# Sliding-window attention on Trainium2: from three float32r passes over 128-query blocks to plain float32 on four 64x64 tiles, with halves of 64 queries and 192 keys

## The chip, the cores and the metric

The kernel runs on one core of a Trainium2 chip. The time is device microseconds of one execution; the median of three runs of the kernel before is 2179.53 us (2178.03 to 2180.18).

The engines are called as in the profile: PE (TensorE; PEld is its loading of weights), DVE (VectorE), ACT (ScalarE), POOL (GpSimd) and SP (SyncE). Each works through its own instructions in order and waits for the others by semaphores.

## What is computed

A decoder layer over 2048 tokens of width 1024: one input product, then dilated window attention (16 heads of 64) beside a Mamba-2 mixer, an output product over both and a layer norm. The change concerns attention:

```python
for dilation in (1, 4, 16):          # query t sees t - j*dilation, j = 0..128
    scores = q . k - slope * distance            # q scaled by 1/8
    scores = where(0 <= steps <= 128, scores, -inf)
    lse = logsumexp(scores); p = exp(scores - lse); o = p @ v
y_att = sum over dilations of softmax(lse_1, lse_4, lse_16) * o
```

With dilation r the tokens fall into r subsequences, and each is cut into blocks of 128. A query sees at most 128 steps back, so a block of queries needs its own block of keys and the one before it.

## The kernel before, in words

**Products (to about 1250 us).** q, k, the gate z and the mixer's inputs come from one product in which every matmul is float32r with operands split in a high and a low part (three passes), arranged as seven products of 512-column halves; 44 jobs of two column tiles each. A result leaves PSUM by ACT (`ev<-pp`, L319) or DVE (L327), in tiles of the pool `ev` (six buffers), and `fin_qk` (L361) ends q and k: ACT rounds the scaled value into `hi` (L366), DVE forms the remainder (L367), and SP stores both (L369, L370) to `d_qh`, `d_ql`, `d_kh`, `d_kl`. The mixer's work is threaded between the products by the table `later`, keyed on a count of products. `copy_v` (L493) reorders V in DRAM for dilations 4 and 1 through POOL's queue, a token's row at a time.

**Attention (1250 to 1757 us).** Everything goes in pairs of heads: head h of a pair lies on partitions 64h to 64h+63. For each of 8 pairs, three dilations (d = 0 is dilation 16, d = 1 is 4, d = 2 is 1), four groups `qd` and two halves make 24 steps; a step takes two blocks of 128 queries for both heads. 192 steps in all. The order is written by hand (`manual_schedule`): in iteration i each engine gets `scores` of step i, `transposes` of step i-2 (TA = 2) and `values` of step i-3, then the odd jobs of that place.

- `scores` (L792): per block, q as weights of 64 rows and 128 columns, k as moving data of 256 columns (128 for a `first` block, which has no block before it: all of d = 0, the first of each subsequence otherwise), three passes (high-high, high-low, low-high) for two heads, into the banks `S` (pool `psS`, four). DVE then adds the bias table and takes the row minimum (L824), ACT exponentiates with the row sum (L832).
- `transposes` (L843): 128x128 pieces of P, four per key block, through the two banks `T` (`psT`), and one DVE copy (L854) per four into `PT`.
- `values` (L858): v as weights of 128 rows and 64 columns per head, PT moving, 128 columns; both heads side by side in a bank `N` (`psN`, two buffers), one bank for the four blocks of a group; ACT copies it to `num` when the group's second half is done (L877, L879, L882).
- `statistics` (L885) transposes minima and sums through an `N` bank after a dilation's end, `gather` and `weights` form the softmax over dilations, `combine` (POOL, for the last pair DVE) adds up.

q for d = 1 and d = 2 is permuted by POOL (`permute`, L773: high and low part, four pieces each). `load_qk` (L745) loads four arrays of 1 MB a pair on POOL's queue, `load_dil` (L753) the bias table (SP) and V (POOL). In the first four iterations `warm` (L836) adds eight matmuls on PE.

**Output (from 1757 us).** The product of both branches, split in high and low parts, four rows of tokens of the mixer's half first, then attention's half. Its weights are loaded by `load_w` on POOL's queue into buffers of attention as they come free.

Of the kernel before, what the change touches and what calls it, by code (L numbers as in the profile page):

```python
# [28 lines left out]
def hybrid_layer(ctx, tc, xT, xc, w52, wv, convw, convb, dtb, alog, dskp, gcol, wout,  # L29
# [15 lines left out]
    d_qh = [dtile(f"d_qh{i}", [128, S]) for i in range(8)]  # L45
    d_ql = [dtile(f"d_ql{i}", [128, S]) for i in range(8)]
    d_kh = [dtile(f"d_kh{i}", [128, S]) for i in range(8)]
    d_kl = [dtile(f"d_kl{i}", [128, S]) for i in range(8)]
# [37 lines left out]
    with ExitStack() as c1:  # L86
# [274 lines left out]
        def fin_qk(p, i, scale):  # L361
            dh, dl = (d_kh, d_kl) if scale == 1.0 else (d_qh, d_ql)

            def f(ci, q, e):
                hi = ev.tile([128, 512], F32R, name="ev")
                nc.scalar.activation(hi, e, AF.Copy, scale=scale)  # L366
                nc.vector.scalar_tensor_tensor(e, e, scale, hi.bitcast(F32), op0=OP.mult, op1=OP.subtract)  # L367
# [125 lines left out]
        def copy_v(d, b):  # L493

            o = (b % 4 * 512 + b // 4 * 32, 8 * b)[d - 1]
            nc.gpsimd.dma_start(d_v[d][b], dap(d_v[0], o * D, [[128 * D, (4, 16)[d - 1]], [D, (32, 8)[d - 1]], [1, D]]))
# [153 lines left out]
        with tc.manual_schedule(engines={E.PE, E.DVE, E.Activation, E.Pool}):  # L650
# [13 lines left out]
            for m, (ph, (kind, i)) in enumerate(jobs):  # L664
# [34 lines left out]
                elif kind == "z":  # L699
                    fin = fin_z(p, i)  # L700
                else:
                    fin = fin_qk(p, i, -0.125 if kind == "q" else 1.0)
# [23 lines left out]
    with ExitStack() as c2:  # L726
        qk = [c2.enter_context(tc.tile_pool(name="qk0", bufs=1, side="right", reuse_waits="tile"))]
        qq = c2.enter_context(tc.tile_pool(name="qq", bufs=1, side="right", reuse_waits="tile"))
        qk.append(c2.enter_context(tc.tile_pool(name="qk1", bufs=1, side="right", reuse_waits="tile")))
# [9 lines left out]
        def load_pair(pr):  # L739

            A = {"pr": pr, "num": [], "tab": {}, "v": {}, "q": {0: []}, "k": []}
# [3 lines left out]
        def load_qk(A):  # L745
            pr = A["pr"]
            for x, src, to in (("qh", d_qh, A["q"][0]), ("kh", d_kh, A["k"]),
# [95 lines left out]
        def transposes(d, qd, half, P):  # L843
            pts = {}
            for which in (0, 1):
                bl = [b for b in range(2) if which or not first(d, qd, 2 * half + b)]
                if not bl:
                    continue
# [410 lines left out]
```

## Time and profile before

| what | value |
|---|---|
| median of three runs | 2179.53 us |
| span of the profiled execution | 2166.2 us (mean granted clock 0.976) |
| outside the span (median less span) | 13.3 us |
| attention, first scores to last values | about 507 us of the span, 62.5 us a pair |
| PE busy in the whole span | 2045.6 us (94%) |
| DMA | 525.26 MB, mean 242 GB/s |

The median is of executions timed from outside; the profile gives the span from the first to the last instruction of one execution. The difference stands for what lies around it.

How to read the rows: a group (`--` by line) reads `line engine op out<-in shapes xcount | busy us, mean ns of one | idle before, what ended it`. A timeline row reads `start us, duration us, engine line op out<-in shapes xcount [idle before <- what ended it]`, and equal instructions that follow each other are merged, so the time from one row's start to the next tells more than a duration: a matmul's end is modelled, and it overlaps the next. A row of waits reads `engine line waited for: us in total, times, longest us`.

### The profile page before, as it was taken

Reading aid. Unit: us, or ns where it says so; the run is one execution under the profiler, and the core shown is the slowest. Engines: PE = TensorE matmul, PEld = TensorE weight load, DVE = VectorE, ACT = ScalarE, POOL = GpSimd, SP = SyncE. Lnnn points to the kernel's source line nnn. Section 1 sums busy time; section 2 is a strip of 40 time slices with the busy share of each in tenths; the row PEclk is TensorE's granted clock in tenths of the full one; section 3 lists DMA queues with packets and bytes.
Section 4 is the critical chain, followed back from the end, with each engine's and each line's share of the span. In section 5 each row is a group of like instructions: output and inputs, shape, how many; then the busy total and the mean of one; then the engine's idle time right before and its main releaser. Section 6 shows DMA issues by size and latency. Waiting matters only on the chain.

```text
span 2166.2 us, 38916 instructions
## 1 busy us (share of the span) xinstructions
PE 2045.6 (94%) x13856; PEld 1701.3 (79%) x13856; DVE 1393.9 (64%) x3145; ACT 1153.7 (53%) x3007; POOL 1089.8 (50%) x899
## 2 busy tenths in 40 slices
PE   7999998989999999979999999999999977999998
PEld 7998777768787787858888878788877865888886
DVE  3431554558999677735555568888888845655655
ACT  4231444435555676645766578888888841222221
POOL 2122545657687666655555331776566670422222
PEclk9999989999999999989999999999999988999999
DMA  9999778977678888898889863777776799222220
GB/s 330 373 334 339 231 256 283 326 282 225 190 223 292 307 319 299 286 399 285 278 281 289 290 233 94 226 217 225 231 224 184 206 367 283 98 102 84 97 82 29
DMA packets 260802, 525.26 MB, mean 242 GB/s; under 512 B 43713, under 2 KB 122689, under 8 KB 244609
## 3 DMA queue, kind: packets, MB, share of 16 engines
q1 hardware_dynamic: 181984, 255.37, 36.9%
q0 software_dynamic: 35280, 184.30, 24.0%
q10 hardware_dynamic: 43344, 83.12, 11.9%
q8 instruction: 109, 1.79, 0.3%
q14 instruction: 85, 0.69, 0.1%
HBM read 346.15 MB, written 193.33 MB: 249 GB/s over the span
## 4 chain that ended last, share of the span: by engine, by line
PE 47%; DMA 8%; DVE 4%; ACT 3%; issue 1%; ACTq 0%; POOL 0%; SPq 0%; DVEq 0%; POOLq 0%
PE S L816 6%; PE N L872 6%; PE T L852 6%; PE S L1032 4%; PE pp L310 3%; PE S L1034 3%; PE S L1033 3%; PE pp L314 3%; PE pp L312 3%; PE T L1032 2%; PE T L1033 2%; PE T L1034 2%; DMA kl<-d_kl 1%; DMA wb<-d_wd 1%; DVE P L824 1%
## 5 line engine op out<-in xcount | busy, mean ns | idle before, releaser
L266 POOL TENSOR_TENSOR w<-wr,w 128x512 fp32r<-128x512 f32 x231 | 353.8, 1548 | 183.9 <-ACT w L265 133.5
L832 ACT ACTIVATE P<-P,st 128x256 f32<-128x256 f32 (+1 forms) x768 | 345.1, 451 | 90.6 <-DVE st L824 90.1
L824 DVE CUSTOM_DVE_ANT_0 P<-S,tb 128x256 f32<-128x256 f32 (+1 forms) x768 | 235.4, 362 | 72.5 <-PE S L816 39.7
L319 ACT COPY ev<-pp 128x512 f32<-128x512 f32 x176 | 102.4, 582 | 184.2 <-PE pp L314 120.3
L854 DVE COPY PT<-T 128x512 f32<-128x512 f32 (+1 forms) x304 | 196.4, 677 | 4.0 <-PE T L852 4.0
L852 PE MATMUL T<-ident,P 128*128 128x128 f32 x1200 | 175.1, 282 | 6.0 <-DVE PT L854 6.0
L872 PE MATMUL N<-PT,v 128*64 128x128 f32 x2400 | 173.2, 281 | 0.0
L265 ACT CAST w<-wr 128x512 fp32r<-128x512 f32 x231 | 138.0, 618 | 51.9 <-DVE wr L258 35.1
L258 DVE TENSOR_TENSOR wr<-wr 128x512 f32<-128x512 f32 x132 | 143.1, 1084 | 15.2 <-POOL w L266 6.2
L872 PEld LDWEIGHTS N<-PT,v 128*64 128x64 f32 x2400 | 127.1, 136 | 32.1 <-issue 22.8
L852 PEld LDWEIGHTS T<-ident,P 128*128 128x128 f32 x1200 | 127.6, 140 | 30.0 <-DVE PT L854 7.4
L939 POOL TENSOR_TENSOR wb<-num,wb 128x2048 f32<-128x2048 f32 x21 | 96.3, 4587 | 98.6 <-DMA wb<-d_wd 54.5
L832 ACT ACTIVATION_READ_ACCUMULATOR P<-P,st 128x1 f32 x768 | 143.9, 187 | 0.0
L327 DVE TENSOR_TENSOR ev<-pp,ev 128x512 f32<-128x512 f32 x152 | 100.6, 682 | 54.1 <-PE pp L314 45.0
L816 PE MATMUL S<-kh,qp 64*128 64x256 f32 (+1 forms) x1024 | 124.4, 303 | 0.0
L1009 DVE TENSOR_REDUCE tb<-P 128x128 f32<-128x1024 f32 x32 | 64.0, 2000 | 85.2 <-PE N L1038 49.2
L416 DVE SCALAR_TENSOR_TENSOR acc<-U,cw,acc 128x2048 f32<-128x2048 f32 x36 | 111.2, 3089 | 4.5 <-ACT acc L413 4.1
L367 DVE SCALAR_TENSOR_TENSOR ev<-ev 128x512 f32<-128x512 f32 x64 | 64.2, 1015 | 66.6 <-ACT ev L366 66.6
L150 PE MATMUL pp<-vh,xh 128*128 128x256 f32 (+1 forms) x320 | 90.2, 289 | 15.1 <-ACT xh L173 15.0
L816 PEld LDWEIGHTS S<-kh,qp 64*128 64x128 f32 x1024 | 87.3, 185 | 21.5 <-issue 20.4
L143 POOL TENSOR_TENSOR vl<-vraw,vh 128x256 fp32r<-128x256 f32 (+1 forms) x32 | 30.1, 943 | 129.7 <-ACT vh L142 107.5
L1071 POOL TENSOR_TENSOR kh<-kh,wb 128x1024 f32<-128x1024 f32 x8 | 19.2, 2399 | 142.7 <-DVE kh L1070 142.7
(370 smaller groups left out, 6139.1 us busy)
## 6 DMA issues: line engine op xcount, KB each, us to landing
wr<-w ACTq DMA_DIRECT2D x157, 256.0 KB
v<-d_v POOLq DMA_DIRECT2D x24, 1024.0 KB, 7.1
wb<-d_wd SPq DMA_DIRECT2D x48, 512.0 KB
d_wc<-w SPq DMA_DIRECT2D x44, 512.0 KB
w<-d_wc POOLq DMA_DIRECT2D x44, 512.0 KB, 6.4
csb<-d_cs ACTq DMA_DIRECT2D x32, 512.0 KB
st<-xT SPq DMA_DIRECT2D x31, 512.0 KB
d_v<-vt SPq DMA_DIRECT2D x16, 512.0 KB
```

Of the source, the lines that this page charges most:

```text
L258: tt = lambda o, a, b, op=OP.subtract: nc.vector.tensor_tensor(q[o], q[a], q[b], op=op)
L265: nc.scalar.copy(t[:, 0], q[nm])
L266: nc.gpsimd.tensor_tensor(t[:, 1], q[nm], t[:, 0].bitcast(F32), op=OP.subtract)
L416: return lambda: nc.vector.scalar_tensor_tensor(acc[0], U[:, j:j + 16, :], cw[:, i, j:j + 1], acc[0], op0=OP.mult, op1=OP.add)
L816: nc.tensor.matmul(ov(sp[h][:, 256 * b:256 * b + w]), A["q"][d][x][hr, blk], kv(A["k"][y][hr]), start=(m == 0), stop=(m == 2))
L824: nc.vector.tensor_tensor_reduce(P[:, h, b, 256 - w:256], sp[h][:, c0:c0 + w], tab[:, h, tab.shape[2] - w:], 1.0, 3.0e38, OP.add, OP.min, ...
L832: nc.scalar.activation(p, p, AF.Exp, bias=stat(A, 0, d, h, blk), scale=-1.0, accum_out=stat(A, 1, d, h, blk))
L852: nc.tensor.transpose(tp[:, h, b], P[:, h, b, 128 * which:128 * which + 128], ident)
L854: nc.vector.tensor_copy(pt[:, :, bl[0]:2], tp[:, :, bl[0]:2])
L872: nc.tensor.matmul(nm[64 * h:64 * h + 64, bq * 128:bq * 128 + 128], v[:, k, 64 * h:64 * h + 64], pts[which][:, h, b], start=(f or not whic ...
L1032: nc.tensor.matmul(ps, uh[:, e, :], wh, start=(e == 0), stop=False)
L1033: nc.tensor.matmul(ps, uh[:, e, :], wl, start=False, stop=False)
```

## The change

q and k stay plain float32: `fin_qk` stores what the product gives, once, and the factor -1/8 is applied by DVE's bias instruction instead (its scale, with tables multiplied by -8). A pair loads two arrays, q and k, both double buffered, and POOL permutes one q per dilation.

A block of 128 queries is taken as two halves of 64. A half sees 192 keys: for the first half the two half blocks before it and its own, and likewise for the second. So the two halves see different windows, and each (head h, half a) gets its own 64x64 tile of PE: rows by h, columns by a. A step now takes blocks `half` and `2 + half` of a group instead of two neighbours; in the second of them the 192 columns lie at the other end of P (`cols`), so that the last 64 keys of the first and the first 64 of the second stand next to each other in columns 128 to 255 and are transposed together. That is four transposes of 128 keys and, in steps with a block of two key blocks, two of these shared ones, with a copy of half the width into `PC`. Values follow in two groups: 128 keys with 128 rows and 64 columns per head, moving 64 columns; then the remaining 64 keys on four tiles (rows by block, columns by head). Since a window begins at half blocks, V is also needed shifted by 64 rows: `vs`, loaded beside `v`, 15 blocks of it.

N becomes two banks, `N0` and `N1`, one for each of the step's blocks, used by a group of two steps and copied by two ACT copies of 256 columns, with one buffer each. The statistics are transposed through `T`. Within a subsequence block the tokens are reordered by half blocks, in `permute`, `copy_v` (pieces of 16 or 4 rows), the tables and the statistics. `load_w` names other buffers.

On PE a full step of attention (dilation 4) stood as follows; S are scores, T the transposes, N the values, kh and kl the parts of k, qp the permuted q, PT the transposed P:

```order
L816 MATMUL S<-kh,qp 128x4x2x32 x2
L816 MATMUL S<-kl,qp 128x4x2x32 x2
L816 MATMUL S<-kh,qp 128x4x2x32 x4
L816 MATMUL S<-kl,qp 128x4x2x32 x2
L816 MATMUL S<-kh,qp 128x4x2x32 x2
L852 MATMUL T<-ident,P 128x128 x8
L872 MATMUL N<-PT,v 64x128 x8
```

and stands now, in the same place (ex is the permuted q, PC the shared transposes, the two N the two banks):

```order
L812 MATMUL S<-k,ex 64x192 x8
L839 MATMUL T<-ident,P 128x128 x4
L847 MATMUL T<-ident,P 128x128 x2
L865 MATMUL N_13177<-PT,v 64x64 x2
L865 MATMUL N_13177<-PT,vs 64x64 x2
L865 MATMUL N_13178<-PT,vs 64x64 x2
L865 MATMUL N_13178<-PT,v 64x64 x2
L865 MATMUL N_13177<-PC,v 64x64 x2
L865 MATMUL N_13178<-PC,vs 64x64 x2
L865 MATMUL N_13177<-PC,vs 64x64 x2
L865 MATMUL N_13178<-PC,v 64x64 x2
```

Twelve score matmuls became eight, eight transposes six, and eight value matmuls sixteen of half the columns.

On ACT, at the end of dilation 4 and the beginning of dilation 1, the exponentials (P), the copies of N and that of the statistics (sT) stood like this:

```order
L879 COPY num<-N 128x16x32
L832 ACTIVATE P,st<-P,st 128x256 x8
L879 COPY num<-N 128x16x32
L892 COPY sT<-N 128x128
L832 ACTIVATE P,st<-P,st 128x256 x8
L882 COPY num<-N 128x4x16x8
```

and stand now:

```order
L892 COPY num<-N_17422 128x2x2x4x16
L892 COPY num<-N_17423 128x2x2x4x16
L824 ACTIVATE P,st<-P,st 128x192 x8
L892 COPY num<-N_17529 128x2x2x4x16
L892 COPY num<-N_17530 128x2x2x4x16
L907 COPY sT<-T 64x128
L908 COPY sT<-T 64x2x4x16
L824 ACTIVATE P,st<-P,st 128x192 x8
L895 COPY num<-N_17649 128x4x16x4
L895 COPY num<-N_17650 128x4x16x4
```

The exponentials keep their number at three quarters of the width, and each copy of N became two.

The core of the diff:

```diff
-        def fin_qk(p, i, scale):
-            dh, dl = (d_kh, d_kl) if scale == 1.0 else (d_qh, d_ql)
-
+        def fin_qk(p, i, to):
             def f(ci, q, e):
-                hi = ev.tile([128, 512], F32R, name="ev")
-                nc.scalar.activation(hi, e, AF.Copy, scale=scale)
-                nc.vector.scalar_tensor_tensor(e, e, scale, hi.bitcast(F32), op0=OP.mult, op1=OP.subtract)
-                s = slice(512 * (2 * p + q), 512 * (2 * p + q) + 512)
-                nc.sync.dma_start(dh[i + ci][:, s], hi.bitcast(F32))
-                nc.sync.dma_start(dl[i + ci][:, s], e)
+                s = 512 * (2 * p + q)
+                nc.sync.dma_start(to[i + ci][:, s:s + 512], e)
             return f
...
-        psN = c2.enter_context(tc.tile_pool(name="psN", bufs=2, space=PSUM, reuse_waits="tile"))
+        psN = c2.enter_context(tc.tile_pool(name="psN", bufs=1, space=PSUM, reuse_waits="tile"))
...
             v = A["v"][d] = io.tile([128, 16, 128], F32, name="v", bufs=3)
-            nc.gpsimd.dma_start(v, d_v[d][:, :, pr * 128:pr * 128 + 128].rearrange("b p e -> p b e"))
+            rows = lambda o, n, p: dap(d_v[d], o * D + pr * 128, [[D, p], [128 * D, n], [1, 128]])
+            nc.gpsimd.dma_start(v, rows(0, 16, 128))
+            if d:
+                vs = A["vs"][d] = io.tile([128, 16, 128], F32, name="vs", bufs=3)
+                nc.gpsimd.dma_start(vs[:, 0:15], rows(64, 15, 128))
...
+        def cols(d, qd, half, i):
+
+            w = 128 if first(d, qd, 2 * i + half) else 192
+            return slice(384 - w, 384) if i else slice(0, w)
...
+            for i in range(2):
+                blk, cs = 4 * qd + 2 * i + half, cols(d, qd, half, i)
+                for h in range(2):
+                    for a in range(2):
+                        o, kv = sp[h][64 * a:64 * a + 64, cs], keys(A, d, qd, 2 * i + half, h, a)
+                        if d:
+                            o = o.rearrange("p (c r j) -> p c r j", r=kv.shape[2], j=kv.shape[3])
+                        nc.tensor.matmul(o, A["q"][d][64 * h:64 * h + 64, blk, 64 * a:64 * a + 64], kv,
+                                         start=True, stop=True)
             for h in range(2):
...
+                    nc.vector.tensor_tensor_reduce(P[:, h, cs], sp[h][:, cs], t, -0.125, 3.0e38, OP.add, OP.min,
+                                                   accum_out=stat(A, 0, d, h, blk))
...
         def transposes(d, qd, half, P):
...
+            tp = psT.tile([128, 2, 2, 128], F32, name="T")
+            for h in range(2):
+                for i in range(2):
+                    nc.tensor.transpose(tp[:, h, i], P[:, h, 256 * i:256 * i + 128], ident)
+            pt = io.tile([128, 2, 2, 128], F32, name="PT", bufs=4)
+            nc.vector.tensor_copy(pt, tp)
+            new = [i for i in range(2) if not first(d, qd, 2 * i + half)]
+            if not new:
+                return pt, None
+            tc_ = psT.tile([128, 2, 2, 128], F32, name="T")
+            for h in range(2):
+                nc.tensor.transpose(tc_[:, 0, h], P[:, h, 128:256], ident)
+            pc = io.tile([128, 2, 128], F32, name="PC", bufs=2)
...
+                A["N"] = [psN.tile([128, 512], F32, name=f"N{i}") for i in range(2)]
...
+                for a in range(2):
+                    for h in range(2):
+                        w = (v, vs)[a != i][:, m - (a == i == 0 or a != i), 64 * h:64 * h + 64]
+                        mm(out(i, h, 64 * a, 64 * a + 64), w, pt[:, h, i, 64 * a:64 * a + 64], half == 0 and a == 0)
+            for a in range(2):
+                for i in range(2):
+                    m, rows = at(2 * i + half), slice(64 * i, 64 * i + 64)
+                    if first(d, qd, 2 * i + half):
+                        continue
+                    for h in range(2):
+                        w = v[rows, m - i] if a == i else vs[rows, m - 2 * i]
+                        mm(out(i, h, 64 * a, 64 * a + 64), w[:, 64 * h:64 * h + 64],
+                           pc[rows, h, 64 * a:64 * a + 64], False)
             if half == 1:
...
-            ps = psN.tile([128, 512], F32, name="N")
+            ps = psT.tile([128, 512], F32, name="T")
```

In the short steps, where `first` holds for both blocks, the scores are eight matmuls of 128 columns, the transposes four as before, and the values four matmuls of 128 columns as before.

More of the change, by code (lines that the diff above doesn't have):

```diff
@@ L43, in dtile @@
         return dram.tile(shape, F32, name=name, tag=name)
[L45 to L48, printed above, removed]
+    d_q = [dtile(f"d_q{i}", [128, S]) for i in range(8)]
+    d_k = [dtile(f"d_k{i}", [128, S]) for i in range(8)]
     d_za = [dtile(f"d_za{i}", [128, S]) for i in range(8)]
@@ L838, in warm @@
             ps = psT.tile([128, 512], F32, name="T")
[L839 to L840 removed]
+            x = A["k"]
+            for n in range(2):
                 nc.tensor.matmul(ps, x[:, 0, :], x[:, 4:8, :].rearrange("p r j -> p (r j)"), start=True, stop=True)
         def transposes(d, qd, half, P):
[L844 to L848, printed above, removed]
[L849 to L856 removed]
+            tp = psT.tile([128, 2, 2, 128], F32, name="T")
+            for h in range(2):
+                for i in range(2):
+                    nc.tensor.transpose(tp[:, h, i], P[:, h, 256 * i:256 * i + 128], ident)
[8 more added lines that the diff above has]
+            pc = io.tile([128, 2, 128], F32, name="PC", bufs=2)
+            rows = slice(64 * new[0], 128)
+            nc.vector.tensor_copy(pc[rows], tc_[rows, 0])
+            return pt, pc
         def values(A, d, qd, half, pts):
+            pt, pc = pts
             if half == 0:
@@ L862, in values @@
                     A["num"].append(cm_.tile([128, NR, NJ], F32, name="num", bufs=6))
-                A["N"] = psN.tile([128, 512], F32, name="N")
-            nm, num, v = A["N"], A["num"][d], A["v"][d]
-            for b in range(2):
-                bq = 2 * half + b
-                blk = 4 * qd + bq
-                f = first(d, qd, bq)
-                kb = blk - 4 if d == 1 else blk - 1
-                for k, which in ((blk, 1),) if f else ((kb, 0), (blk, 1)):
-                    for h in range(2):
-                        nc.tensor.matmul(nm[64 * h:64 * h + 64, bq * 128:bq * 128 + 128],
-                                         v[:, k, 64 * h:64 * h + 64], pts[which][:, h, b],
-                                         start=(f or not which), stop=bool(which))
@@ new lines, in values, with mm @@
+            num, v, vs = A["num"][d], A["v"][d], A["vs"].get(d)
+            at = lambda bq: 4 * bq + qd if d == 1 else 4 * qd + bq
+            out = lambda i, h, lo, hi: A["N"][i][64 * h:64 * h + 64, 128 * half + lo:128 * half + hi]
+            def mm(o, l, r, start):
+                nc.tensor.matmul(o, l, r, start=start, stop=True, skip_group_check=True)
+            for i in range(2):
+                m = at(2 * i + half)
+                if first(d, qd, 2 * i + half):
+                    for h in range(2):
+                        mm(out(i, h, 0, 128), v[:, m, 64 * h:64 * h + 64], pt[:, h, i], half == 0)
+                    continue
[3 more added lines that the diff above has]
+                        mm(out(i, h, 64 * a, 64 * a + 64), w, pt[:, h, i, 64 * a:64 * a + 64], half == 0 and a == 0)
@@ new lines, in values @@
+            for a in range(2):
+                for i in range(2):
+                    m, rows = at(2 * i + half), slice(64 * i, 64 * i + 64)
+                    if first(d, qd, 2 * i + half):
+                        continue
+                    for h in range(2):
+                        w = v[rows, m - i] if a == i else vs[rows, m - 2 * i]
+                        mm(out(i, h, 64 * a, 64 * a + 64), w[:, 64 * h:64 * h + 64],
+                           pc[rows, h, 64 * a:64 * a + 64], False)
@@ L1168, in hybrid_layer @@
                     residual(3)
-                    for e, name in enumerate(("num", "num", "num", "num", "qp", "v", "wb", "wb")):
+                    for e, name in enumerate(("num", "num", "num", "num", "vs", "v", "wb", "wb")):
                         load_w(e, name)
```

177 lines of the change are left out of this document (77 added, 100 removed).

## The prediction

> **What bounds the kernel now.** I read the page's first part, then the busy time in four stretches of the program, and then, inside the stretch that the change rewrites, the timeline of PE. The page:
>
> ```profile
> PE 2045.6 (94%) x13856; PEld 1701.3 (79%) x13856; DVE 1393.9 (64%) x3145; ACT 1153.7 (53%) x3007; POOL 1089.8 (50%) x899
> ```
>
> The stretches are the part of the products in which q and k are made and the state-space mixer runs (640 to 1000), attention (1250 to 1757), and the output stage. The columns are the stretch, its length, and busy time with instructions of PE, PEld, DVE, ACT and POOL, then granted clock, DMA share and GB/s.
>
> ```profile
> 640.00:1000.00 360.00, 333.22 (x1695) 271.63 (x1693) 246.82 (x336) 223.79 (x440) 233.41 (x184) 0.97 0.89 313
> 1250.00:1757.00 507.00, 499.96 (x5924) 407.07 (x5922) 428.15 (x1897) 411.65 (x1656) 308.74 (x232) 1.00 0.71 211
> 1757.00:2166.00 409.00, 372.53 (x1634) 301.82 (x1633) 222.98 (x276) 91.00 (x129) 104.60 (x53) 0.96 0.40 129
> ```
>
> PE fills 500 of attention's 507 us, at full clock, with DVE and ACT at 428 and 412: PE sets the pace, and a cheaper PE step meets the other two soon. In the products PE stands still for 360 - 333 = 27 us. What a step of attention costs on PE is read from its timeline: first two consecutive groups of a step in which all blocks have only their own keys (128 wide), then one in which both blocks have two key blocks.
>
> ```profile
> 1459.74 0.66 PE L852 MATMUL T<-ident,P 128*128 128x128 f32 x4
> 1460.33 0.66 PE L872 MATMUL N<-PT,v 128*64 128x128 f32 x8
> 1460.92 0.33 PE L816 MATMUL S<-kh,qp 64*128 64x128 f32 x2
> ...
> 1461.73 0.66 PE L852 MATMUL T<-ident,P 128*128 128x128 f32 x4
> ...
> 1473.60 0.39 PE L816 MATMUL S<-kh,qp 64*128 64x256 f32 x2
> 1473.83 0.28 PE L816 MATMUL S<-kl,qp 64*128 64x256 f32 x2
> 1473.95 0.40 PE L816 MATMUL S<-kh,qp 64*128 64x256 f32 x4
> 1474.18 0.28 PE L816 MATMUL S<-kl,qp 64*128 64x256 f32 x2
> 1474.30 0.28 PE L816 MATMUL S<-kh,qp 64*128 64x256 f32 x2
> 1474.51 1.09 PE L852 MATMUL T<-ident,P 128*128 128x128 f32 x8
> 1475.53 1.09 PE L872 MATMUL N<-PT,v 128*64 128x128 f32 x16
> 1476.56 0.39 PE L816 MATMUL S<-kh,qp 64*128 64x256 f32 x2
> ```
>
> The short step lasts 1461.73 - 1459.74 = 1.99 us, the full one 1476.56 - 1473.60 = 2.96: scores 0.91, transposes 1.02, values 1.03. Comparing four transposes (0.59) with eight (1.02) gives 0.1075 each and a fixed 0.16 for changing from one kind of work to the next; the values give 0.44 for eight more instructions, 0.055 each, and a fixed 0.15; the scores' pairs follow each other at 0.117, which leaves a fixed 0.21. An f32 matmul is two instructions here (x8 where the code has four). How many run side by side is seen by comparing with a full-width f32 matmul of the mixer:
>
> ```profile
> 1096.21 1.05 PE L561 MATMUL ss<-bc,H 128*128 128x128 f32 x8
> 1097.19 0.33 PE L570 MATMUL ss<-mt,xdt 128*64 128x128 f32 x2
> ```
>
> There eight instructions of 128 columns take 0.98, (0.98 - 0.16)/8 = 0.10 each. The values' instructions stream the same 128 columns at half of that, so their two column halves (heads h = 0, 1) work abreast; the scores' pairs show the same for two row halves. Streaming costs 0.1075/128 = 0.84 ns a column and instruction.
>
> By the counts of the softmax rows there are 432/2 = 216 blocks of two key blocks and 336/2 = 168 of one:
>
> ```profile
> L832 ACT ACTIVATE P<-P,st 128x256 f32<-128x256 f32 x432 | 214.3, 498 | 51.5 <-DVE st L824 51.0
> L832 ACT ACTIVATE P<-P,st 128x128 f32<-128x128 f32 x336 | 130.8, 391 | 39.1 <-DVE st L824 39.1
> L879 ACT COPY num<-N 128x512 f32<-128x512 f32 x32 | 18.0, 564 | 0.0
> L854 DVE COPY PT<-T 128x512 f32<-128x512 f32 x296 | 193.7, 684 | 4.0 <-PE T L852 4.0
> ```
>
> By the code's rule for first blocks that is 104 full steps, 80 short ones and 8 mixed.
>
> **The change, part by part. Scores.** Twelve matmuls of 256 columns in six rounds of two become eight f32 matmuls, 16 instructions, of 192 columns. If the four tiles of a round (two row halves, two column halves) work abreast, that is four rounds of 192 x 0.84 = 0.161 us: 0.65. No row shows four tiles abreast; the near rows show two, in either direction, so the cost lies between four rounds (0.65) and eight (1.29). I take four: both halvings work by themselves at full rate. In short steps it is four rounds of 0.1075, 0.43, for 0.81 - 0.21 = 0.60 now (1460.92 to 1461.73).
>
> **Transposes.** Two fewer in each full step: 6 x 0.1075 = 0.645 for 0.86. Nothing replaces them in short steps.
>
> **Values.** Now eight matmuls of 128 columns, 0.88 in all. After: first eight of 64 columns over the shared 128 keys, 16 instructions two abreast, 8 rounds of 64 x 0.84 = 0.054, 0.43; then eight of 64 columns over 64 keys on four tiles, 4 rounds, 0.215. Whether a round of 64 columns can be so short depends on the weights, which must be loaded meanwhile:
>
> ```profile
> L872 PEld LDWEIGHTS N<-PT,v 128*64 128x64 f32 x2400 | 127.1, 136 | 32.1 <-issue 22.8 <-DVE st L824 7.9 <-DVE mm L920 1.0
> L561 PEld LDWEIGHTS ss<-bc,H 128*128 128x128 f32 x240 | 31.4, 191 | 2.3
> ```
>
> 64 more columns of weights lengthen the load by 0.055 us, so a load of 64 just fits under a round of 64, as a load of 128 fits under 128 columns at L561. Bounds: 0.054 and 0.1075 a round; I take 0.054, since L561 is the same balance. The second group changes the tiles once more (another 0.15), but the scores behind it use the same four tiles, so their 0.21 falls to some 0.07 (bounds 0 and 0.21). Fixed costs together: 0.16 + 0.15 + 0.15 + 0.07 = 0.53, as now (0.16 + 0.15 + 0.21 = 0.52).
>
> A full step on PE: 0.65 + 0.645 + 0.43 + 0.215 + 0.53 = 2.47, against 2.96: 0.49 less. A mixed one, worked out likewise, saves about 0.5. A short one has 0.43 + 0.07 + 0.14 (no second group, so the scores' whole fixed 0.21 stays) + 0.59 + 0.59 = 1.82.
>
> **Who is next.** ACT: four exponentials of 192, halfway between 391 and 498, 0.445 each, and per step one copy of 256 columns of N (two for every two steps, in place of one of 512). Between half of 0.564 and all of it I take 0.36. Full step 1.78 + 0.36 = 2.14, under 2.47. Short step 4 x 0.391 + 0.36 = 1.92, over PE's 1.82: there ACT becomes the bound and only 0.07 of 1.99 is won. DVE now starts a 256-wide piece of the scores every 0.345 us and copies twice:
>
> ```profile
> 1475.07 0.42 DVE L824 CUSTOM_DVE_ANT_0 P<-S,tb 128x256 f32<-128x256 f32 x1
> ...
> 1475.41 0.42 DVE L824 CUSTOM_DVE_ANT_0 P<-S,tb 128x256 f32<-128x256 f32 x1
> ...
> 1476.10 1.28 DVE L854 COPY PT<-T 128x512 f32<-128x512 f32 x2
> ```
>
> Even at the old 0.345 for 192 columns, four pieces, one copy (0.64) and one of half the width (0.4) make 2.42: hidden under PE's 2.47.
>
> **The waits it adds.** N was double buffered and is now two banks used once each: the first values of the next group of four blocks wait for ACT's copies, and behind them on PE stand the next scores, on which DVE and then ACT wait. ACT copied soon after the values ended at 1476.56:
>
> ```profile
> 1477.17 0.57 ACT L879 COPY num<-N 128x512 f32<-128x512 f32 x1
> ```
>
> 0.6 us later, so two copies are done 0.6 + 0.72 = 1.3 us after the values end, and the next values come after scores and transposes, 0.72 + 0.80 = 1.5: hidden by 0.2. The statistics' 16 transposes move into the two T banks and wait there for DVE's copy. The nearest wait of that kind:
>
> ```profile
> 1469.42 0.66 PE L852 MATMUL T<-ident,P 128*128 128x128 f32 x4 [0.79 <-DVE PT L854]
> ```
>
> So 0 to 0.8 each; I take 0.3, 5 us in all. POOL's queue keeps seven loads a pair (two of q and k, three of V, two of shifted V, for four and three) and loses half of the permutation, so loads are issued no later; the copies that reorder V keep number and bytes. The warming matmuls cost the same (eight f32r for two f32 of four times the time).
>
> **Products.** Evicting q and k loses this work and half of its stores:
>
> ```profile
> L367 DVE SCALAR_TENSOR_TENSOR ev<-ev 128x512 f32<-128x512 f32 x64 | 64.2, 1015 | 66.6 <-ACT ev L366 66.6
> L366 ACT ACTIVATE ev<-ev 128x512 fp32r<-128x512 f32 x64 | 39.6, 629 | 35.4 <-DMA d_qh<-ev 16.3 <-DMA d_kh<-ev 14.0 <-DVE ev L327 2.2
> ACT ev L366 <- DMA d_qh<-ev: 13.1, 5, 6.6
> ACT ev L319 <- DMA d_kl<-ev: 7.9, 2, 4.7
> ```
>
> DVE and ACT are not the bound there (247 and 224 of 360 us), so only PE's 27 us of standing still can shrink, and the mixer's own chain holds part of it. Bounds 0 and 27; the last two rows, ACT's waits for such stores in that stretch, make up 21 us between them, not all of it on PE's path: I take 10.
>
> **Output stage.** POOL sends the first loads for it after a chain that begins in the last pair; PE waits for them, and later for that pair's softmax weights:
>
> ```profile
> 1727.12 4.58 POOL L939 TENSOR_TENSOR wb<-num,wb 128x2048 f32<-128x2048 f32 x1 [16.93 <-ACT P L832]
> 1754.44 1.41 POOL L984 DMA_DIRECT2D num<-d_uh x2
> 1765.67 0.79 PE L1032 MATMUL S<-kh,num 128*128 128x512 f32 x1 [6.52 <-DMA num<-d_uh]
> 1820.10 0.59 PE L1038 MATMUL N<-one,tb 128*128 128x1 f32 x2 [15.70 <-DVE tb L1009]
> ```
>
> POOL is busy from 1727 on whatever PE does, so 14 quicker steps after that lengthen the first wait by up to 14 x 0.49 = 7 us. The second wait, 15.7, ends with a chain that starts at the end of attention and moves with it; it takes up the 7. Cost nothing; 7 if that cover were gone.
>
> **The sum.** 104 x 0.49 + 80 x 0.07 + 8 x 0.5 = 51 + 5.6 + 4 = 60.6; less 5 for the statistics, and 10 from the products: 65.6. The profiled span is 2166.2 and the median of the runs 2179.53, so 13.3 lie around it: 2166.2 - 65.6 + 13.3 = 2114.
>
> **The rivals.**
>
> Two abreast, not four. The code writes the two instructions of one tile behind each other and the four tiles in turn; if PE follows no more than two tiles at a time, the scores take 1.29 and the values' second group 0.43: a full step 2.47 + 0.645 + 0.215 = 3.33, a short one 1.82 + 0.43 = 2.25. 104 x 0.37 + 80 x 0.26 = 59 more, plus 5, less 10: 2234, slower. It decides where fewer than about 2.5 tiles run abreast: a share f more rounds costs 104 x 0.86f + 80 x (0.43f - 0.10), and 65.6 is used up at f = 0.6, n = 4/1.6. For it: no row shows four. Against it: rows and columns of tiles each pair up at full rate. [...] Chance 0.13.
>
> PE's instruction rate. A full step will have 16 + 6 + 32 = 54 matmul instructions, each with a load of weights, where 12 + 8 + 16 = 36 take 2.96 us now. The fastest that a row shows is the values' 0.055 each, the rate kept up over a whole step 0.082. If they cannot be fed faster than 0.055, a full step takes 54 x 0.055 = 2.97 and gains nothing, a short one (28 x 0.055 = 1.54) stays with ACT: 5.6 - 5 + 10 = 11 less, 2169; at 0.082 it would be 4.43 and far slower, and from 0.057 on the 11 are used up. Against it: streaming explains both rates as well. [...] Chance 0.11, mostly near the upper side of 0.057: 0.03 faster, 0.03 the same, 0.05 slower.
>
> ACT and the single N banks. If a copy of half the width costs the full 0.564, a short step has 1.56 + 0.56 = 2.13 on ACT, 0.21 x 80 = 17 us worse than reckoned, and in full steps the copies are done 0.6 + 1.13 = 1.73 after the values, 0.23 late every second step, 52 x 0.23 = 12: a gain of 37, 2143. Against it: the exponentials' times fall with the width. Chance 0.10.
>
> **How the numbers follow.** My forecast, four abreast, has 0.66. About 0.2% (4 us) can be told from no change. Faster: 0.66 + 0.10 + 0.03 = 0.79; the same 0.03; slower 0.13 + 0.05 = 0.18. The time is the forecast's, 2114. Its low end: no fixed cost before the scores (7 less), all 27 us of the products (17 less), a copy at half of 0.564 (6 less): 2084, put at 2085. Its high end: rounds of 64 columns at 0.1075 in both value groups, 104 x 0.65 = 68 more: 2181. The range goes on to 2200 to hold the third case and the near half of the second. It leaves out two abreast, the far half of the second, and a little at the lower edge: 0.13 + 0.05 + 0.02 = 0.20.
>
> **What would show it.** In the changed profile: scores of a full step from first to last instruction near 0.65 + 0.1, and 0.72 to the first transpose; six transposes 0.80; values 0.43 + 0.22 + 0.3; a full step 2.47, a short one 1.92 with ACT without gaps. Scores of 1.3 us mean two abreast; phases that stretch in proportion to their instructions mean the feeding rate; waits of the values for ACT's copy of N mean the banks. PE's idle time before attention should fall by some 10. I am wrong if a full step is not below 2.96, or if it is and the output stage grows by what attention saved.

## The result and the profile after

The changed kernel takes 2242.6 us (median of four runs, 2241.5 to 2243.5) against 2178.8: a ratio of 1.0296, 95% interval 1.0282 to 1.0311. It is slower by 3%, where faster was forecast. The profiled execution spans 2239.4 us, at a mean granted clock of 0.949 for 0.976.

First the engines' totals of the changed kernel:

```profile
PE 2023.7 (90%) x16128; PEld 1644.7 (73%) x16128; DVE 1286.6 (57%) x3081; ACT 1106.1 (49%) x3047; POOL 1050.8 (47%) x867
```

PE has 22 us less work in 73 us more. Where it waits is seen by stages. The products of the kernel before, with the columns of the prediction's stretches:

```profile
209.00:1250.00 1041.00, 982.64 (x4767) 803.38 (x4768) 674.67 (x859) 590.52 (x1107) 637.39 (x561) 0.97 0.83 282
```

and products, attention and output of the changed one:

```profile
210.00:1312.00 1102.00, 999.41 (x4768) 815.05 (x4768) 618.96 (x796) 557.60 (x1043) 619.71 (x559) 0.95 0.74 250
1312.00:1828.00 516.00, 459.05 (x8225) 336.99 (x8224) 375.66 (x1898) 397.00 (x1759) 289.40 (x201) 0.94 0.72 212
1828.00:2239.00 411.00, 373.21 (x1601) 301.92 (x1601) 223.47 (x274) 91.02 (x130) 102.83 (x54) 0.95 0.40 126
```

Two losses show. The products, from which the change took work, grew by 61 us: PE idles 1102 - 999 = 103 us there, for 58. In attention PE's work fell by 41 us (500 to 459), but its idle time rose from 7 to 57, so the stage lasts 516 for 507. The output stage is as before within 3 us.

What a step costs is what the prediction said. On PE's timeline of the changed kernel, first the beginnings of two short steps that follow each other, then a full step and the first row of the next:

```profile
1440.57 0.67 PE L812 MATMUL S<-k,q 64*64 64x128 f32 x16
...
1442.35 0.67 PE L812 MATMUL S<-k,q 64*64 64x128 f32 x16
...
1468.57 0.83 PE L812 MATMUL S<-k,ex 64*64 64x192 f32 x16
1469.34 0.66 PE L839 MATMUL T<-ident,P 128*128 128x128 f32 x4
1469.83 0.38 PE L847 MATMUL T<-ident,P 128*128 128x128 f32 x2
1470.14 0.34 PE L865 MATMUL N<-PT,v 128*64 128x64 f32 x4
...
1471.04 0.83 PE L812 MATMUL S<-k,ex 64*64 64x192 f32 x16
```

Scores take 0.77 (foretold 0.72), transposes 0.80 (0.80), values 0.90 (0.95), the full step 1471.04 - 1468.57 = 2.47 (2.47), the short one 1.78 (1.92; the 55 like it take 1.86 on average). Four tiles do work abreast: with two, by the prediction's estimate, the scores alone would have taken 1.29.

**The products: what became late.** The waits between 210 and 800 us in the changed kernel:

```profile
POOL U L387 <- DMA d_xs<-U: 40.9, 6, 11.1
PE pp L308 <- ACT ev L317: 40.6, 10, 9.1
PE pp L312 <- POOL w L264: 30.9, 8, 8.0
DVE wr L256 <- DMA wr<-w: 28.0, 8, 6.3
ACT wot L115 <- DMA woraw<-wout: 19.8, 6, 6.2
```

and two of the same stretch before (209 to 800):

```profile
PE pp L310 <- ACT ev L319: 24.4, 9, 7.6
DVE wr L258 <- DMA wr<-w: 5.9, 3, 3.6
```

Transfers of every kind come late: the raw weights for DVE (28.0 us for 5.9), and with them POOL's low parts of weights and PE. Of the transfers in this stage the change touches two kinds: the stores of q and k, which became half as many, and the copy that reorders V. The copy's issues and landing times, before and after:

```profile
L496 POOL DMA_DIRECT2D d_v<-d_v x32: 514/574/821, 223.7 to 677.3; - x32
DMA to landing us min/median/max: 3.5/7.4/13.2
```

```profile
L489 POOL DMA_DIRECT2D d_v<-d_v x32: 557/630/839, 224.7 to 747.0; - x32
DMA to landing us min/median/max: 12.6/14.3/17.7
```

Number and bytes are the same, and for the first sixteen copies so are the packets, 64 KB each; the others have 32 KB before and 16 KB now (runs of rows are joined, so the copies did not go a row at a time in either). What differs throughout is how many move at once. Before, the 64 KB packets of the first copy start four together (227.96 to 228.60 us, then 230.87 to 231.48); now they start in twos (229.54 and 229.56, 232.11 and 232.13), 2.4 us each. In the first copy of the other sixteen, sixteen packets start from 510.10 to 511.77 us before; now again two at a time (546.77 and 547.08, 547.94 and 548.07). The access pattern's outermost dimension went from 4 and 16 row groups to the 2 halves of 64 queries, and as many packets as it has entries start together in these copies. My theory A, which the rows alone don't show: for about 10 us each (the first from 229.54 to 239.70), two of the core's 16 DMA engines are blocked, and every other transfer that has a share on them lands late.

**Attention: two kinds of waits.** The changed kernel's attention, PE's and one of DVE's:

```profile
DVE mm L930 <- DMA cm<-d_st: 32.0, 6, 10.4
PE N L865 <- ACT num L889: 33.4, 9, 10.6
PE N L865 <- issue: 10.6, 5, 2.7
PE S L812 <- issue: 4.4, 3, 3.1
PE T L903 <- issue: 2.6, 1, 2.6
PE T L847 <- issue: 2.4, 1, 2.4
```

The 33.4 us fall at the start of a pair, and the one behind them is DVE's wait for the statistics of the pair before (`weights`): in one of the six, DVE stands still for 9.91 us until L930 runs at 1458.45, and the score reductions (L818, from 1459.08) and the copy of T (L841, 1460.19) come behind it. Why the statistics are late, SP's queue tells, with the ACT copy that makes them and the POOL multiply ahead:

```profile
1435.86 0.26 ACT L908 COPY sT<-T 64x128 f32<-64x128 f32 x1
...
1436.29 4.57 POOL L971 TENSOR_TENSOR wb<-wb 128x2048 f32<-128x2048 f32 x1
...
1440.89 0.36 SPq L972 DMA_DIRECT2D d_ua<-wb  x1
1441.34 6.34 SPq L917 DMA_DIRECT2D d_st<-sT  x4
1451.98 0.38 SPq L923 DMA_DIRECT2D cm<-d_st  x1
```

The statistics lie ready at 1436.1, but `d_ua`, the store of the gated output of the pair before, stands ahead of them and waits for POOL until 1440.9. In the kernel before, the same store came after them, and so it did in each of the six pairs that wait now:

```profile
1449.99 1.97 SPq L900 DMA_DIRECT2D d_st<-sT  x4
1455.99 0.38 SPq L906 DMA_DIRECT2D cm<-d_st  x1
1456.42 0.54 SPq L955 DMA_DIRECT2D d_ua<-wb  x1
```

That is theory C. Why the order turned round is not shown: SP is not among the engines whose order is written by hand (`manual_schedule` names PE, DVE, ACT and POOL), so its order was made when the kernel was built. The other 20 us (10.6 + 4.4 + 2.6 + 2.4) are pauses put to "issue", nine of them over 0.9 us, many in the midst of like instructions:

```profile
1407.53 0.28 PE L865 MATMUL N<-PT,v 128*64 128x64 f32 x3
1410.54 0.22 PE L865 MATMUL N<-PT,v 128*64 128x64 f32 x1 [2.72 <-issue]
```

A transfer of the queue q8, 16 KB of kind "instruction", starts at 1407.84, just when PE stopped, and takes 1.26 us; ahead of the other eight pauses such a transfer starts too, 0.0 to 1.9 us before PE stops. Attention's transfers on q8 before and after:

```profile
q8 instruction: 47, 0.77, 0.6%
```

```profile
q8 instruction: 64, 1.05, 0.9%
```

PE runs 8225 matmuls and 8224 weight loads there, 257 a transfer, and 5924 + 5922 before, 252: I read the transfers as pages of about 256 of PE's instructions. A full step has 108 of these, so by estimate a page now lasts 2.47 x 256/108 = 5.9 us. In the 8 us ahead of each of the nine, 122 to 210 packets of 8 KB and 0.6 us each start on queue q1, most of them of the combining weights (`wb`, 3 MB a pair). Of the 64 pages, the seven with the most such packets in the 8 us ahead of them (197 to 212) all go with a pause, of the next four (138 to 180) two do, and of the other 53 none. Theory E: the next page is behind these. If theory E is right, that costs 20 us in 516 here.

### The profile page after: what moved, and what is told of

It is laid out like the page before. It is cut to its first block, busy times and chain, and to the rows that moved or that the text cites. A ratio compares the mean times of both kernels' runs of the same rounds, so it can differ in the third digit from the quotient of the medians.

```text
span 2239.4 us, 43053 instructions
## 1 busy us (share of the span) xinstructions
PE 2023.7 (90%) x16128; PEld 1644.7 (73%) x16128; DVE 1286.6 (57%) x3081; ACT 1106.1 (49%) x3047; POOL 1050.8 (47%) x867
## 4 chain that ended last, share of the span: by engine, by line
PE 50%; DMA 9%; ACT 3%; DVE 2%; issue 1%; SPq 1%; POOL 0%; ACTq 0%; DVEq 0%; POOLq 0%
PE N L865 6%; PE pp L308 5%; PE pp L310 5%; PE pp L312 5%; PE S L812 4%; PE S L1051 3%; PE T L839 3%; PE S L1053 3%; PE S L1052 3%; DMA d_st<-sT 2%; ACT P L824 2%; PE T L1051 2%; PE T L1052 2%; PE T L1053 2%; DMA cm<-d_st 1%
## 5 line engine op out<-in xcount | busy, mean ns | idle before, releaser
L824 ACT ACTIVATE P<-P,st 128x192 f32<-128x192 f32 (+1 forms) x768 | 322.1, 421 | 73.4 <-DVE st L818 68.9
L818 DVE CUSTOM_DVE_ANT_0 P<-S,tb 128x192 f32<-128x192 f32 (+1 forms) x768 | 207.2, 325 | 98.9 <-PE S L812 77.1
L865 PE MATMUL N<-PT,v 128*64 128x64 f32 (+1 forms) x1536 | 129.3, 266 | 39.8 <-ACT num L889 33.4
L865 PEld LDWEIGHTS N<-PT,v 128*64 128x64 f32 x1536 | 80.8, 141 | 75.2 <-ACT num L889 43.0
L841 DVE COPY PT<-T 128x512 f32<-128x512 f32 x192 | 131.7, 686 | 4.5 <-PE T L839 4.3
L839 PE MATMUL T<-ident,P 128*128 128x128 f32 x768 | 130.8, 295 | 0.2 <-DVE PT L841 0.2
L812 PE MATMUL S<-k,ex 64*64 64x192 f32 (+1 forms) x2048 | 116.1, 337 | 4.6 <-issue 4.4
L308 PE MATMUL pp<-TT3h,w 128*128 128x512 f32 x176 | 73.9, 420 | 19.3 <-ACT ev L317 19.1
L149 PE MATMUL pp<-vl,xh 128*128 128x256 f32 (+1 forms) x320 | 90.7, 287 | 0.0
L312 PE MATMUL pp<-TT2h,w 128*128 128x512 f32 x176 | 71.7, 407 | 16.9 <-POOL w L264 16.9
```

What stands on the lines that cost most here:

```text
L308: nc.tensor.matmul(ps, w[:, 0, k], th[:, k], start=start and k == 0, stop=False, skip_group_check=not start)
L312: nc.tensor.matmul(ps, w[:, 1, k], th[:, k], start=False, stop=(k == 3), skip_group_check=not start)
L812: nc.tensor.matmul(o, A["q"][d][64 * h:64 * h + 64, blk, 64 * a:64 * a + 64], kv, start=True, stop=True)
L818: nc.vector.tensor_tensor_reduce(P[:, h, cs], sp[h][:, cs], t, -0.125, 3.0e38, OP.add, OP.min, accum_out=stat(A, 0, d, h, blk))
L824: nc.scalar.activation(p, p, AF.Exp, bias=stat(A, 0, d, h, blk), scale=-1.0, accum_out=stat(A, 1, d, h, blk))
L839: nc.tensor.transpose(tp[:, h, i], P[:, h, 256 * i:256 * i + 128], ident)
```

## The experiments

For every ratio below, the kernel before ran again on the same chip as the kernel that it is compared with.

**The copies of V as wide as before** (changed kernel, one edit):

```diff
-nc.gpsimd.dma_start(d_v[d][b], dap(d_v[0], o * D, [[j * D, 2], [128 * D, r], [1, j * D]]))
+nc.gpsimd.dma_start(dap(d_v[d], b * 128 * D, [[j * D, r], [64 * D, 2], [1, j * D]]),
+                    dap(d_v[0], o * D, [[128 * D, r], [j * D, 2], [1, j * D]]))
```

> The changed kernel with one edit: the 32 copies that reorder V walk the same bytes with the row groups outermost (4 for the first 16 copies, 16 for the others) instead of the two halves of 64 queries. Theory A (the copies use as many DMA engines as their outermost dimension has entries, so the change put each on two engines, and every weight load that has a share on these two waits for it): the copies land in about 5 to 7 us instead of 14, the product stage gives back its 60 us, attention starts near 1245 us instead of 1312, and the time is about 2180. Rival B (the loss in the products comes from the removed split of q and k, which moved the order of ACT and VectorE): nothing changes, 2242, attention still starts near 1312.

2159.9 us, ratio to before (2176.3) 0.9937, interval 0.9910 to 0.9965. Its products:

```profile
210.00:1232.00 1022.00, 976.99 (x4768) 801.88 (x4768) 629.59 (x797) 556.86 (x1044) 626.89 (x559) 0.98 0.80 269
```

80 us shorter than with the narrow copies: 58 less idle time of PE, and 22 less busy time for the same matmuls, at a granted clock of 0.98 instead of 0.95. DVE's wait for raw weights is 13.0 us for 28.0, the copies land in 7.3 us at the median. The packets are the changed kernel's (64 and 16 KB), so their size isn't what counts. The time is 20 us under the 2180 foretold: the stage gave back more than its 60, and is now 19 us shorter than the 1041 of the kernel before.

**The narrow copies in the kernel before** (`[[j * D, 2], [128 * D, r], [1, j * D]]` there; its attention then reads V in another order, in the same number of bytes):

> The kernel before with one edit: its 32 copies of V take the changed kernel's outermost dimension of two (the rows of V then stand in another order than its attention takes, the same number of bytes moves). Theory A: the product stage grows by some 60 to 66 us, the time is about 2240, and the copies land in about 14 us. Rival B: 2179, the product stage unchanged.

2251.8 us, ratio 1.0362 (1.0330 to 1.0394). Its products and copies:

```profile
210.00:1332.00 1122.00, 1003.86 (x4768) 817.39 (x4768) 664.80 (x860) 592.89 (x1108) 634.30 (x561) 0.94 0.77 261
```

```profile
DMA to landing us min/median/max: 12.6/14.0/16.4
```

1122 us for 1041: 81 more from this one line, the mirror of the 80 above. Rival B has nothing left. That the width of the copies is the cause is shown; that two blocked engines are the way by which others are late stays my reading, since a packet's row names its queue and not its engine. The loads of `U` agree: issued on POOL's queue, they land in 6.0 us at the median before and 8.8 after, in 5.8 with wide copies in the changed kernel and in 8.5 with narrow ones in the kernel before.

**The store of the gated output on POOL's queue** (changed kernel, one edit):

```diff
-            nc.sync.dma_start(dap(d_ua, pr * 128, ...
+            nc.gpsimd.dma_start(dap(d_ua, pr * 128, ...
```

> The changed kernel with one edit: the store of a pair's combined and gated output is issued on POOL's queue, behind the multiply that it stores, instead of on SP's. Theory C (in SP's queue this store waits for POOL and holds up the stores of the softmax statistics behind it, so the statistics return late, VectorE waits for them in its queue, and TensorE waits for VectorE): VectorE's waits for the statistics (32 us in six pairs) go to under 5 us, TensorE's six stalls at a pair's change (33 us) go, and the time is about 2210. Rival D (the statistics are late because POOL's chain of combining is itself too slow for the shorter pair): the waits stay over 20 us and the time stays above 2230.

2198.6 us, ratio 1.0108 (1.0072 to 1.0143), 44 less than the changed kernel. Its attention, and PE's and DVE's waits there:

```profile
1313.00:1789.00 476.00, 448.32 (x8210) 328.06 (x8208) 376.18 (x1898) 395.96 (x1759) 290.31 (x203) 0.98 0.76 225
```

```profile
PE N L865 <- issue: 12.1, 7, 3.3
PE N L865 <- ACT num L889: 3.5, 8, 1.1
DVE mm L930 <- DMA cm<-d_st: 1.0, 1, 1.0
```

33.4 us fell to 3.5 and 32.0 to 1.0: theory C, and rival D falls. The last row but one also shows what the single buffers of N cost in this run, at most these 3.5 us.

**Both** (the first sixteen copies now as two transfers with 16 rows outermost, `[[D, 16], [128 * D, 4], [1, D]]`):

> The changed kernel with both causes taken away: the 32 copies of V have an outermost dimension of 16 (the first 16 copies as two transfers each), and the store of a pair's gated output is on POOL's queue. Theories A and C together, if their costs add: 2242.6 less 83 (measured for the copies with 4 and 16 entries outermost) less 44 (the store) is 2116, and up to 10 us less since the first 16 copies now spread over all engines; attention starts near 1225 us and lasts 476. Rival: the two share their gain (a pair that runs faster meets the same DMA queue), and the sum is only partly reached, 2130 to 2150.

> The kernel with both causes taken away again, without further edits, on the chip of the run with the gate's load on POOL, so that the two can be compared: 2106 as measured before, 2100 to 2115; if the added edits are worth something, it is 10 to 20 us above that run.

2106.3 us, ratio 0.9684 (0.9645 to 0.9724), and on another chip 2106.8, 0.9694 (0.9670 to 0.9718). The gains add: 83 and 44, and the remaining 9 are what the products gain from the wider first copies (1022 to 1013). That those spread over all engines, as the expectation has it, no row shows; their halves land in 5.3 us at the median. Products and attention of the first:

```profile
212.00:1225.00 1013.00, 974.49 (x4767) 802.07 (x4768) 633.91 (x796) 556.85 (x1044) 627.11 (x575) 0.98 0.81 271
1225.00:1708.00 483.00, 452.90 (x8226) 331.87 (x8224) 374.79 (x1898) 395.58 (x1760) 291.94 (x205) 0.97 0.75 223
```

**Wide copies in the kernel before** (its first sixteen on 16 rows outermost instead of 4):

> The kernel before with one edit: its first 16 copies of V, whose outermost dimension has 4 entries, are each made as two transfers with 16 entries outermost (the other 16 have that already). Theory A says that width is what counts, from 2 to 4 to 16: these copies land in about 3 to 5 us instead of 7 to 13, and the first stretch of the products gains 3 to 12 us, 2165 to 2173. Rival: four engines were already enough, 2176.

2156.8 us, ratio 0.9917 (0.9884 to 0.9950), 17 less than the kernel before and more than foretold: 2, 4 and 16 are an order. It is also the fair partner for the change: products

```profile
211.00:1236.00 1025.00, 978.38 (x4768) 802.31 (x4768) 679.06 (x860) 591.03 (x1107) 647.55 (x577) 0.98 0.85 286
```

against 1013 of both fixes (1006 when measured again): plain q and k are worth 12 to 19 us there, as they were with copies of 4 and 16 (1022 for 1041).

**The pauses.** Five runs aim at theory E. First, in the changed kernel, POOL loads the combining weights of a dilation one multiply ahead (its queue in place of SP's):

> The changed kernel with one edit: the three 1 MB loads of combining weights of a pair are issued on POOL's queue, one ahead of the multiply that needs it, instead of all six halves at once on SP's. Theory E (TensorE's nine pauses of 1 to 3 us inside a group of like matmuls, 20 us in all, which the profile puts to issue, are its instruction page arriving late behind these loads): the pauses fall below 5 us in all, the instruction pages start before TensorE stops, and the time is about 2222. Rival F (the pauses are a limit of TensorE's own queue at over 40 instructions in 1 us): they stay at about 20 us, 2242.

2253.5 us, and PE's pauses still 14.4 us in all. It decides nothing: the first two loads, 2 MB, still leave together, and the statistics, still behind the store in SP's queue, became later (DVE waits 48.7 us). Then, on top of both fixes, smaller pieces:

```diff
-                for h in range(2):
-                    nc.sync.dma_start(f2(wb[64 * h:64 * h + 64]),
-                                      dap(d_wd[pr], (d * 2 + h) * S, [[0, 64], [1, S]]))
+                for c in range(4):
+                    for h in range(2):
+                        nc.sync.dma_start(f2(wb[64 * h:64 * h + 64])[:, 512 * c:512 * c + 512],
+                                          dap(d_wd[pr], (d * 2 + h) * S + 512 * c, [[0, 64], [1, 512]]))
```

> The kernel with both causes taken away, and one edit more: each combining weight is loaded in four pieces of 512 columns (2 KB runs, 24 issues a pair on SP's queue instead of 6), so that fewer and smaller packets stand in the DMA queues at a time. Theory E (TensorE's instruction page comes late because it stands behind the 8 KB packets of these loads, 0.61 us each): the pauses put to issue in attention fall from about 20 us to under 6, and the time is 12 to 18 us below the kernel with both causes taken away. Rival F (TensorE's own queue): the pauses stay, and the time is the same or a few us more for the longer SP queue.

2125.4 us, slower by 19, though the pauses are gone. PE's waits:

```profile
PE S L818 <- DMA k<-d_k: 20.6, 6, 6.8
PE S L1058 <- DMA num<-d_uh: 17.2, 1, 17.2
PE N L871 <- issue: 0.6, 1, 0.6
```

The 24 pieces take 17 us to issue, and the next pair's k, asked for behind POOL's first multiply, leaves while they still load, 12 to 13 us ahead of its pair, and takes as long to land (13 to 17 us ahead, and 10 to 12 to land, without the pieces). So k was asked for ahead of it (`load_qk` moved to the step (0, 3, 1)), with pieces for the first six pairs only, and, as a control, with whole loads:

> The kernel with both causes taken away, and two edits more: the combining weights of the first six pairs are loaded in four pieces of 512 columns, and the next pair's q and k are asked for before POOL's first combining multiply instead of behind it. Theory E: no pause put to issue is left (22 us in 9 pauses without the pieces), k is no longer late (20 us in 5 waits with the pieces alone), TensorE's idle time in attention falls from 30 to under 12 us, attention lasts 460 to 465 us, and the time is 15 to 22 us below the kernel with both causes taken away, 2085 to 2092. Rival F, now that the pieces alone removed the pauses: TensorE only had time to fetch because it waited for k; then the pauses come back, and the time stays near 2106.

> The kernel with both causes taken away, and one edit more: the next pair's q and k are asked for before POOL's first combining multiply instead of behind it; the combining weights stay whole. Theory E: the pauses put to issue stay, 15 to 25 us in all, since the 8 KB packets stay, and the time is 2100 to 2110. Rival F (earlier q and k are what helps): the pauses go, as in the run with the pieces.

The control keeps its pauses (22 us in all) and takes 2112 to 2153 us, a spread that I can't explain (ratio 0.9794 without the longest). With pieces the pauses are 2.6 us, k is in time, and rival F falls: whole loads pause, pieces don't, whether or not k is waited for. The pieces are smaller and also spread over 17 us of issuing instead of 4, and no run separates the two. Yet the kernel takes 2100.1 us, ratio 0.9665 (0.9642 to 0.9688), which the intervals do not tell from both fixes alone. PE is idle for 30 us as before, since another wait took the place:

```profile
PE T L845 <- ACT sT L914: 13.5, 5, 3.7
```

The statistics have one buffer (`sT`), and their stores were now behind the gate's load in SP's queue. That load moved to POOL's queue as well:

> The kernel with the pieces and the earlier q and k, and one edit more: the load of a pair's gate is issued on POOL's queue, ahead of the third combining multiply, instead of on SP's, where it waits for a buffer of POOL with the first part of the statistics' stores behind it. If what stands ahead of the statistics in SP's queue is still what costs (ACT waits 24 us for the single statistics buffer, TensorE 13.5 us for ACT): these waits go to under 3 us, TensorE's idle time in attention falls from 30 to about 15 us, and the time is 2082 to 2092. Rival: POOL's chain pays for the added issue and load (up to 6 us a pair) and the time stays at 2095 to 2105.

2107.6 us, ratio 0.9698 (0.9677 to 0.9719), beside 2106.8 for both fixes on the same chip: nothing won. The waits for `sT` are gone, but PE waits 22.8 us for ACT, and what goes with that is new (last section).

**The order of the tiles** (both fixes; the loop over the two blocks moved inside those over the tiles, so that a tile's matmuls follow each other in the program):

> The kernel with both causes taken away, and one edit more: the eight score matmuls of a step are issued tile by tile (both blocks of one tile, then the next tile) instead of going round the four tiles twice. Theory G (TensorE starts matmuls in program order, and one whose tile is still busy holds up those behind it): the four tiles hardly overlap, the scores of a full step take 2.1 to 2.6 us instead of 0.77, and the kernel is over 150 us longer than the kernel with both causes taken away. Rival H (the array takes any matmul of its queue whose tile is free): same time.

2117.5 us, one run, with the same span as the profiled run of both fixes (2115.7). A full step there:

```profile
1399.84 0.89 PE L818 MATMUL S<-k,ex 64*64 64x192 f32 x16
1400.66 0.66 PE L845 MATMUL T<-ident,P 128*128 128x128 f32 x4
```

0.82 us to the first transpose in place of 0.76, and not 2.1 to 2.6: rival H.

## Why the prediction was wrong

**The step that failed** is in "The waits it adds": "the copies that reorder V keep number and bytes", and so cost nothing. Number and bytes were kept; the width was not. Costed as 0, it measured 61 us net of what the products won, 80 alone. I counted the copies by number and bytes and never asked how many packets of a copy move at once, and so no rival held this case. The rows to see it were there: the copies land in 3.5 to 13.2 us before, and the diff shows the outermost dimension going from 4 and 16 to 2. Neither sign of being wrong that the prediction named came (a full step takes 2.47 us, the output stage is as before), because it looked for them in attention and behind it.

**The second step that failed** is the same sentence's "loads are issued no later". For each queue past which the shorter pair moves things, I had to ask what stands in front. SP's queue holds a store that waits for POOL; before, it came after the statistics, and in the changed kernel it stands in front of them. I suppose that the pair, shorter by some 50/8 = 6 us beside a chain of POOL's that did not shrink, moved it when the kernel was built, but no run shows that. The store in front measured 44 us (two runs).

**The steps that held.** Four tiles abreast: full step 2.47 as predicted. The short step was better, 1.78 to 1.86 for 1.92; a half-width copy of N costs ACT 0.25 from start to start and not 0.36. The N banks cost 1.6 to 4.2 us with the store moved (three runs), the statistics in T about 2 (5 assumed). "Products, I take 10": 12 to 19 at equal width of the copies; the bound of 27 above it was read in 360 of the stage's 1041 us, in which PE stands still for 58. "Output stage, nothing": within 3 us.

**Attention as a whole** was forecast at 507 - 55.6 = 451 us and lasts 474 to 483 with both fixes. Of the difference some 20 us are the pauses, which I had only as a rate of instructions (the second rival, at 0.055 us each; PE starts 54 matmuls in 2.47 us, 0.046 each, so that rival is out), not as a transfer that comes late (theory E). The rest, 3 to 12 us, goes with a granted clock of 0.97 to 0.98 in that stage for 1.00 (PE is busy for 448 to 453 us, 500 - 55.6 = 444 were implied); it isn't separated further.

**The 13.3 us "around the span"** were mostly spread between executions: in the changed kernel's runs span and time differ by 2.1 us (2239.4 and 2241.5). The profiled execution of before was 11 us faster than its median.

That both fixes come to 2106, near the forecast of 2114, is no confirmation of the sum. Measured again, their span is 2098.9 for 2166.2: the products gave 35 us of that (1041 to 1006) where 10 were forecast, and attention 33 (507 to 474) where 55.6 were. That the two misses nearly cancel is luck, and 16 of the 35 are the wider copies, which the kernel before can have as well (1041 to 1025). Against the kernel before with wide copies the change is worth 2156.8 - 2106.3 = 50.5 us, of 65.6 forecast.

**What stays open** is why PE's idle time in attention stays at 26 to 33 us whichever of these waits is taken away.

## What to carry to other kernels

Cost a transfer by the width of its outermost dimension as well as by its bytes: here 32 background copies at a width of 2 made a stage 80 us longer than at 4 and 16. When a stage gets shorter, go through each queue of the changed kernel and look for an entry that waits on an engine that did not get faster, and for what now stands behind it: here one store on SP's queue cost 44 us. When TensorE's instructions become more and smaller, look at the transfers of kind "instruction" beside its pauses: here 47 in 507 us became 64 in 516, nine of them went with pauses of 20 us in all, and with the combining weights loaded in pieces 2.6 us of pauses were left. That these transfers come late is theory E.

## What the runs showed of the hardware that was not expected

**More waits went with a lower clock.** The same products' matmuls took 999 us of PE at a granted clock of 0.95 with 103 us of waits, 977 us at 0.98 with 45. The eight profiles whose products I read in this way (the two kernels, four of the edited ones, both fixes twice) stand in one order throughout, from 36 us of waits, 970 us busy and 0.98 to 118 us, 1004 us and 0.94. That the waits bring the clock down is my reading; no run sets the one without the other.

**Matmuls of different tiles passed each other.** In the run on the tiles' order, in a step with one block of 128 and one of 192 columns, each tile's program order is 128, then 192, tile after tile. In the trace the eight instructions of 128 columns of all four tiles start first (0 to 0.19 us), then the eight of 192 (0.22 to 0.46): the second matmul of the first tile didn't hold up the first of the next. So in this step PE did not keep the program's order, which the text at the start has of every engine.

**A small VectorE operation lasted as long as a GpSimd one.** In the run with the gate's load on POOL, DVE and POOL:

```profile
1470.47 5.39 DVE L936 TENSOR_TENSOR mm<-cm 128x32 f32<-128x32 f32 x1
```

```profile
1471.28 4.52 POOL L982 TENSOR_TENSOR wb<-wb 128x2048 f32<-128x2048 f32 x1
```

With both fixes alone this operation takes 0.18 us. Here five of the eight take 3.8 to 5.4 us, each ending about 0.06 us after POOL's multiply; these five last 22 us together, about the 22.8 that PE waits. In the one shown VectorE's row starts 0.81 us ahead of the multiply (1470.47 and 1471.28), while POOL issued a load. My reading is that the operation was held until the multiply ended, and that the pair's other waits decide whether the two meet. No run shows what holds it.
